# The wide weight sum s75 of block 1's first MLP matrix, made by a plain load and an accumulating DMA instead of VectorE

## The chip, the cores and the metric

The kernel runs on one core of a Trainium2 chip. The metric is the device time of one execution in microseconds (us). The kernel before took 1544.16 us, the median of three executions (1543.84 to 1545.23). Five engines work side by side, each in the order of its own queue: PE (matmul), DVE (VectorE), ACT (ScalarE), POOL (GpSimd) and SP, which here only issues transfers. They wait for each other by semaphores.

## The reference

Two blocks of a small transformer-like model run one after the other on 512 tokens of 1024 channels, each followed by a normalization. Block 1 is a mixer, an attention to a memory and an MLP; block 2 has a sliding-window attention, a convolution and a gated MLP. The part that the change touches is the MLP of block 1:

```
def squared_relu_mlp(h, w1, w2):
    return jnp.square(jax.nn.relu(h @ w1)) @ w2      # w1 1024 x 4096, w2 4096 x 1024
...
x = x + squared_relu_mlp(rmsnorm(x, norm_ffn[l]), ffn_w1[l], ffn_w2[l])
```

All of it is in float32.

## The kernel before, in words

Activations lie transposed, as eight tiles of 128 channels by 512 tokens. A float32 product is made of three products of a narrower format, fp32r: the operand is split into a high part (a cast on ACT) and a low part (the rest, a subtraction on DVE), and PE multiplies high by high, high by low and low by high (`mm3`, lines 459 to 463). The weights come in a fixed order as units of 512 KB, 128 partitions by 1024, eight tiles of 128 by 128. A unit is loaded by SP into a `raw` buffer (four of them; lines 242 and 269), cast by ACT into `whi` (258, 305) and subtracted by DVE into `wlo` (260, 262, 310); there are five buffers each of `whi` and `wlo`, and a cast waits until PE is done with the tile whose buffer it takes.

The first MLP matrix w1 has 16 column pairs. Two are multiplied plainly. The other fourteen, pairs 2 to 15, use Strassen's scheme in Winograd's form, with seven half-sized products in place of eight (`pairg`, `SEVEN`). One pair is two units, r0 and r1 (`wraw[u]` and `wraw[u+1]`). Some of the seven products need sums of blocks of the weights:

- s75 is r0 plus the second half of r1, added to both halves of r0: one DVE instruction on 128 by 1024 (`s75`, line 297), written to a buffer with the tag `sraw`, of which there are two (`NSR`);
- s64, on 128 by 512 twice, is made from s75 and r0 (`s6`, line 315), and from that and r1 (`s4`, line 318), into the other `sraw`.

Then r0 ("a"), s75, s64 and the first half of r1 ("b") are each split into high and low. `seven_steps` lists these operations as six steps. While PE works on an earlier unit, `sevens` hands them out, one step every two tiles of weights (`SPREAD`); what is late is put in by `pairg` at the pair's start. This is the order in which the program is written; where several engines are free to differ, a scheduler sets the order of each engine from it. SP's order is the order of the program.

At a pair's end one product bank is copied by ACT (`c0`, line 380), DVE makes four sums with the PSUM banks into `q` (386 to 389), ACT applies relu and the square (1355, 1356) and casts the result (1358), and DVE makes its low part (1363). The second matrix w2 is multiplied as soon as w1's columns are there. DVE scales its result out of PSUM (1391, `tmp`), and POOL adds it to the running sum (1393, `res+=tmp`).

The pairs are taken so: plain 0 and 1; 2, 3 and 4 together; four columns of w2; pair 5; four of w2; 6, 7 and 8; four of w2; 9; four of w2; 10, 11 and 12; four; 13; four; 14 and 15; eight. Pair 4, 8 and 12 are each the last of three pairs in a row. In the profiled execution this stage runs from 395 to 716 us.

Of the kernel before, what the change touches and what calls it, by code (L numbers as in the profile page):

```python
# [9 lines left out]
F32 = mybir.dt.float32  # L10
# [4 lines left out]
ALU = mybir.AluOpType  # L15
AX = mybir.AxisListType

P = 128
T = 512
D = 1024  # L20

NSLOT = 67
NRAW, NWS = 4, 5

NSR, NQ = 2, 2


SPREAD = [6, 2]
# [140 lines left out]
def _build(ctx, tc, nc, A, out, stage):  # L169
# [8 lines left out]
    def nm(s):  # L178
        cnt[0] += 1
        return f"{s}_{cnt[0]}"  # L180
# [48 lines left out]
    order, seven = weight_order()  # L229
# [44 lines left out]
    def sevens(u, later):  # L274


        if u not in sevp:
            load_raw(u, 1)
            sevp[u] = seven_steps(u)
        n = SPREAD[0] if later else len(sevp[u][1])  # L280
        todo = sevp[u][1]
        for j in range(min(n, len(todo))):
            if later:
                defer(SPREAD[1] * j, lambda todo=todo: todo and todo.pop(0)())
            else:
                todo.pop(0)()

    def seven_steps(u):
        r0, r1 = wraw[u], wraw[u + 1]
        wd = lambda dt, tag, b: wp.tile([P, 1024], dt, tag=tag, bufs=b, name=nm(tag))  # L290
        r3 = r0.rearrange("p (a b) -> p a b", a=2)
        op = {}
        t = {}

        def s75():
            t["s75"] = wd(F32, "sraw", NSR)
            V.tensor_tensor(t["s75"].rearrange("p (a b) -> p a b", a=2), r3,
                            r1[:, T:].unsqueeze(1).to_broadcast([P, 2, T]), op=ALU.add)

        def hi(n, src):  # L300
            def f():
                s = src()
                w = s.shape[-1]
                t[n] = (wd(F32R, "whi", NWS), wd(F32R, "wlo", NWS)) if w > T else (t2(F32R), t2(F32R))
                S.copy(t[n][0], s)  # L305
            return f

        def lo(n, src):
            def f():
                V.tensor_sub(t[n][1], src(), t[n][0].bitcast(F32))  # L310
            return f

        def s6():
            t["s64"] = wd(F32, "sraw", NSR)
            V.tensor_add(t["s64"][:, :T], t["s75"][:, T:], r0[:, :T])

        def s4():
            V.tensor_add(t["s64"][:, T:], t["s64"][:, :T], r1[:, :T])

        def both(*fs):  # L320
            def f():
                for g in fs:
                    g()
            return f

        def end():
            h = lambda n, j: tuple(a[:, j * T:(j + 1) * T] for a in t[n])
            op.update({1: h("a", 0), 4: h("a", 1), 7: h("s75s", 0), 5: h("s75s", 1),
                       6: h("s64s", 0), 3: h("s64s", 1), 2: t["b"]})

        a, b = (lambda: r0), (lambda: r1[:, :T])
        c, d = (lambda: t["s75"]), (lambda: t["s64"])
        return op, [
            both(s75, hi("a", a)),
            both(lo("a", a), hi("s75s", c)),
            both(s6, s4),
            both(lo("s75s", c), hi("s64s", d)),
            both(hi("b", b), lo("s64s", d)),
            both(lo("b", b), end),
        ]  # L340
# [5 lines left out]
    def pairg(name, n1, n2, ops, then, kind="mm"):  # L346
# [11 lines left out]
        wraw.pop(u)  # L358
        wraw.pop(u + 1)
        load_raw(u + 2, 3)  # L360
        if u + 2 in seven:
            sevens(u + 2, True)
        else:
            defer(7, lambda: prefetch(u + 2, 0, 0))
# [77 lines left out]
    def nxt(name, k, n, c=1):  # L442
# [4 lines left out]
        if i % 8 == 0:  # L447
            wraw.pop(u - 1, None)
            wsp.pop(u - 1, None)
            prefetch(u, *PF)  # L450
            if u + 2 in seven and u + 1 not in seven:
                sevens(u + 2, True)
        hi, lo = wsp[u]
# [1415 lines left out]
```

## Time and profile before

| | |
|---|---|
| median of three executions | 1544.16 us |
| the profiled execution | 1543.86 us, of which the span 1542.1 us |
| PE busy | 1514.8 us, 98% of the span |
| DVE busy | 999.0 us, 65% |
| ACT busy | 674.9 us, 44% |
| POOL busy | 143.5 us, 9% |
| loads of weights | 259 of 512 KB, 3.7 us from issue to landing (median) |

The profile is taken from one execution. Busy time is the sum of an engine's instructions, where matmuls that overlap count once; the time between the span and the execution's own time lies before the first and after the last instruction. The chain that ended last is followed back from the last instruction, at each step to what released it. Releasers are worked out from semaphore events: a wait stands under the one that came last.

### The profile page before, as it was taken

The numbers are of one execution on the slowest core, as the hardware profiler recorded it, in microseconds if no ns is written. First come the engines' busy times: TensorE is split into PE (matmuls) and PEld (weight loads), VectorE is DVE, ScalarE is ACT, GpSimd is POOL, SyncE is SP. The second block draws the span as 40 slices with busy tenths as digits, with TensorE's granted clock in tenths as the row PEclk, the third lists the DMA queues.
The fourth block names the chain that finished last, engine by engine and source line by source line (L and its number), as shares of the span: only waits on it lengthen the run. The fifth ranks groups of instructions, "written<-read, shape, count | busy, mean of one in ns | idle before, by whom it ended". The sixth has DMA issues, their size and how long they took to land.

```text
span 1542.1 us, 20324 instructions
## 1 busy us (share of the span) xinstructions
PE 1514.8 (98%) x7904; PEld 1274.9 (83%) x7904; DVE 999.0 (65%) x1623; ACT 674.9 (44%) x1117; POOL 143.5 (9%) x162
## 2 busy tenths in 40 slices
PE   8999999999999999999999999999999999999996
PEld 6888898888888888989888888888888888888886
DVE  6897675554786786767688767335546555555557
ACT  6666555443564353535444444333334331332233
POOL 0002120200201212011400000000020002001101
PEclk9999999999999999999999999999999999999998
DMA  6033335221223323324043222222232222232311
GB/s 254 20 111 100 112 130 197 96 68 55 82 72 106 96 95 109 104 83 137 14 150 131 83 82 83 81 92 92 92 96 96 96 96 96 96 96 92 100 41 56
DMA packets 51505, 149.89 MB, mean 97 GB/s; under 512 B 9552, under 2 KB 14032, under 8 KB 51408
## 3 DMA queue, kind: packets, MB, share of 16 engines
q1 hardware_dynamic: 51264, 148.32, 29.1%
q8 instruction: 62, 1.02, 0.3%
q14 instruction: 35, 0.29, 0.1%
q10 hardware_dynamic: 144, 0.26, 0.1%
HBM read 143.97 MB, written 3.28 MB: 95 GB/s over the span
## 4 chain that ended last, share of the span: by engine, by line
PE 95%; DVE 2%; ACT 2%; issue 1%; DMA 0%; POOL 0%; SPq 0%; DVEq 0%; ACTq 0%; POOLq 0%
PE mm L461 28%; PE mm L462 27%; PE mm L463 27%; PE sm L463 2%; PE sm L461 2%; PE sm L462 2%; ACT whi L258 0%; ACT t L1090 0%; DVE wlo L260 0%; DMA raw<-wts 0%; PE sm L581 0%; PE sm L1576 0%; PE sm L1575 0%; PE sm L1577 0%; PE sm L713 0%
## 5 line engine op out<-in xcount | busy, mean ns | idle before, releaser
L461 PE MATMUL mm<-t,whi 128*128 128x512 f32 (+1 forms) x1888 | 719.9, 381 | 9.1 <-ACT whi L254 7.3
L462 PE MATMUL mm<-t,whi 128*128 128x512 f32 (+1 forms) x1888 | 716.7, 380 | 0.2 <-DVE t L530 0.2
L463 PE MATMUL mm<-t,wlo 128*128 128x512 f32 (+1 forms) x1888 | 716.8, 380 | 0.0
L258 ACT CAST whi<-raw 128x1024 fp32r<-128x1024 f32 x226 | 236.5, 1051 | 432.7 <-PE mm L462 286.2
L461 PEld LDWEIGHTS mm<-t,whi 128*128 128x128 f32 x1888 | 355.3, 188 | 77.9 <-ACT whi L254 7.3
L463 PEld LDWEIGHTS mm<-t,wlo 128*128 128x128 f32 x1888 | 355.3, 188 | 72.1 <-DVE wlo L260 0.8
L462 PEld LDWEIGHTS mm<-t,whi 128*128 128x128 f32 x1888 | 355.2, 188 | 69.6 <-DVE t L530 0.4
L260 DVE TENSOR_TENSOR wlo<-raw,whi 128x1024 fp32r<-128x1024 f32 x219 | 287.4, 1312 | 81.8 <-ACT whi L258 78.8
L575 POOL TENSOR_TENSOR acc<-acc,tmp 128x512 f32<-128x512 f32 (+1 forms) x37 | 52.7, 1432 | 468.2 <-ACT tmp L571 467.9
L1436 DVE TENSOR_TENSOR tmp<-mm,acc 128x512 f32<-128x512 f32 x46 | 31.7, 689 | 48.8 <-PE mm L463 46.8
L1393 POOL TENSOR_TENSOR res<-res,tmp 128x512 f32<-128x512 f32 x24 | 39.0, 1638 | 247.9 <-DVE tmp L1391 217.3
L310 DVE TENSOR_TENSOR wlo<-sraw,whi 128x1024 fp32r<-128x1024 f32 x28 | 38.4, 1375 | 26.5 <-ACT whi L305 26.5
L461 PE MATMUL sm<-t,whi 128*128 128x256 f32 (+1 forms) x176 | 50.4, 286 | 1.8 <-ACT whi L305 1.8
L1676 DVE TENSOR_TENSOR zp<-mm,acc 128x512 f32<-128x512 f32 x22 | 15.2, 691 | 55.0 <-PE mm L463 54.9
L463 PE MATMUL sm<-t,wlo 128*128 128x256 f32 (+1 forms) x176 | 50.4, 286 | 0.0
L462 PE MATMUL sm<-t,whi 128*128 128x256 f32 (+1 forms) x176 | 50.2, 285 | 0.0
L305 ACT CAST whi<-sraw 128x1024 fp32r<-128x1024 f32 x28 | 29.3, 1047 | 45.8 <-PE mm L462 41.0
L1692 POOL TENSOR_TENSOR res<-res,tmp 128x512 f32<-128x512 f32 x16 | 20.7, 1294 | 260.2 <-DVE tmp L1691 260.2
L1679 DVE TENSOR_TENSOR tmp<-tmp,mm 128x512 f32<-128x512 f32 x22 | 15.1, 687 | 43.4 <-PE mm L463 42.6
L1391 DVE TENSOR_TENSOR tmp<-mm,acc 128x512 f32<-128x512 f32 x32 | 21.6, 686 | 26.5 <-PE mm L463 22.6
L1691 DVE TENSOR_TENSOR tmp<-mm,acc 128x512 f32<-128x512 f32 x16 | 11.1, 692 | 39.2 <-PE mm L463 39.2
L461 PEld LDWEIGHTS sm<-t,whi 128*128 128x128 f32 x176 | 33.1, 188 | 2.5 <-ACT whi L305 2.0
(379 smaller groups left out, 1840.2 us busy)
## 6 DMA issues: line engine op xcount, KB each, us to landing
raw<-wts SPq DMA_DIRECT2D x259, 512.0 KB, 3.7
res<-xT SPq DMA_DIRECT2D x16, 256.0 KB, 5.2
yT<-t SPq DMA_DIRECT2D x6, 256.0 KB, 2.3
tmp<-tmp SPq DMA_DIRECT2D x20, 64.0 KB, 2.0
gm<-gm SPq DMA_DIRECT2D x4, 256.0 KB, 5.2
dn<-ch SPq DMA_DIRECT2D x4, 256.0 KB, 2.3
tmp<-memT SPq DMA_DIRECT2D x4, 256.0 KB, 2.6
cst<-const SPq DMA_DIRECT2D x1, 576.0 KB, 6.7
```

Source lines behind the costliest of these rows:

```text
L258: S.copy(hi, r)
L260: defer(LO, lambda r=r, hi=hi, lo=lo: V.tensor_sub(lo, r, hi.bitcast(F32)))
L305: S.copy(t[n][0], s)
L310: V.tensor_sub(t[n][1], src(), t[n][0].bitcast(F32))
L461: PE.matmul(ps, lhsT=ahi, rhs=bhi, start=start, stop=False)
L462: PE.matmul(ps, lhsT=ahi, rhs=blo, start=False, stop=False)
L463: PE.matmul(ps, lhsT=alo, rhs=bhi, start=False, stop=stop)
L575: eng.tensor_add(acc[:, :w], acc[:, :w], dst[:, :w])
L1391: V.tensor_mul(t, ps, rb2)
L1393: G.tensor_add(x[n], x[n], t)
L1436: V.tensor_mul(t, ps, rb)
L1692: G.tensor_add(x[n], x[n], t)
```

## The change

The DVE instruction s75 is taken out. A new function `sums` makes s75 in a buffer of its own tag (two buffers, `NS75`): SP loads unit u a second time, now into s75, and POOL's queue issues a DMA that reads the second half of unit u+1 from memory twice (a broadcast of 512 columns to two halves) and adds it to what is there. `sums` is called where the pair's raw units are first loaded, and ahead of that for the pairs that come next: in `pairg`, after the raw loads, for the next two pairs, and in `nxt` two or three units ahead. `sraw` is left with one buffer, for s64. The pool of 512-column slots has 65 tiles instead of 67, and the scratch space of descriptors for DMAs is doubled.

```diff
--- before.py
+++ after.py
@@ -19,10 +19,10 @@
 T = 512
 D = 1024
 
-NSLOT = 67
+NSLOT = 65
 NRAW, NWS = 4, 5
 
-NSR, NQ = 2, 2
+NSR, NS75, NQ = 1, 2, 2
 
 
 SPREAD = [6, 2]
@@ -276,6 +276,7 @@
 
         if u not in sevp:
             load_raw(u, 1)
+            sums(u)
             sevp[u] = seven_steps(u)
         n = SPREAD[0] if later else len(sevp[u][1])
         todo = sevp[u][1]
@@ -285,17 +286,23 @@
             else:
                 todo.pop(0)()
 
+    sum75 = {}
+
+    def sums(u):
+
+        if u not in sum75:
+            s = wp.tile([P, 1024], F32, tag="s75", bufs=NS75, name=nm("s75"))
+            nc.sync.dma_start(out=s, in_=A["wts"][u])
+            nc.gpsimd.dma_start(out=s.rearrange("p (a b) -> p a b", a=2),
+                                in_=A["wts"][u + 1][:, T:].unsqueeze(1).to_broadcast([P, 2, T]),
+                                accum_op=ALU.add)
+            sum75[u] = s
+
     def seven_steps(u):
         r0, r1 = wraw[u], wraw[u + 1]
         wd = lambda dt, tag, b: wp.tile([P, 1024], dt, tag=tag, bufs=b, name=nm(tag))
-        r3 = r0.rearrange("p (a b) -> p a b", a=2)
         op = {}
-        t = {}
-
-        def s75():
-            t["s75"] = wd(F32, "sraw", NSR)
-            V.tensor_tensor(t["s75"].rearrange("p (a b) -> p a b", a=2), r3,
-                            r1[:, T:].unsqueeze(1).to_broadcast([P, 2, T]), op=ALU.add)
+        t = {"s75": sum75.pop(u)}
 
         def hi(n, src):
             def f():
@@ -331,7 +338,7 @@
         a, b = (lambda: r0), (lambda: r1[:, :T])
         c, d = (lambda: t["s75"]), (lambda: t["s64"])
         return op, [
-            both(s75, hi("a", a)),
+            hi("a", a),
             both(lo("a", a), hi("s75s", c)),
             both(s6, s4),
             both(lo("s75s", c), hi("s64s", d)),
@@ -358,6 +365,9 @@
         wraw.pop(u)
         wraw.pop(u + 1)
         load_raw(u + 2, 3)
+        for v in (u + 2, u + 4):
+            if v in seven:
+                sums(v)
         if u + 2 in seven:
             sevens(u + 2, True)
         else:
@@ -448,6 +458,9 @@
             wraw.pop(u - 1, None)
             wsp.pop(u - 1, None)
             prefetch(u, *PF)
+            for v in (u + 2, u + 3):
+                if v in seven:
+                    sums(v)
             if u + 2 in seven and u + 1 not in seven:
                 sevens(u + 2, True)
         hi, lo = wsp[u]
@@ -1857,7 +1870,7 @@
     from concourse.bass_utils import run_bass_kernel_spmd
 
     arrays = layout(inputs)
-    nc = bacc.Bacc("TRN2", target_bir_lowering=False, num_devices=1, dynamic_dma_scratch_size=1024)
+    nc = bacc.Bacc("TRN2", target_bir_lowering=False, num_devices=1, dynamic_dma_scratch_size=2048)
     A = {n: nc.dram_tensor(n, a.shape, mybir.dt.from_np(a.dtype), kind="ExternalInput").ap()
          for n, a in arrays.items()}
     out = nc.dram_tensor("yT", (8, P, T), F32, kind="ExternalOutput").ap()
```

Lines after the edit are numbered otherwise: 297 is gone, 305 is 312, 310 is 317, 315 is 322, 318 is 325, 386 to 389 are 396 to 399, 1393 is 1406. The new load is line 295, the accumulating DMA line 296. The numbers in names count the tiles of the program, and the same tile can have a number one or two higher.

POOL's queue around pairs 10, 11 and 12 (s75_1152, s75_1170, s75_1175), after the change; `res` lines are the adds of w2's columns.

```order
L1406 TENSOR_TENSOR res_591_2840<-res_591_2840,tmp_1147_5799 128x512
L1406 TENSOR_TENSOR res_592_2842<-res_592_2842,tmp_1153_5836 128x512
L1406 TENSOR_TENSOR res_593_2844<-res_593_2844,tmp_1165_5884 128x512
L1406 TENSOR_TENSOR res_594_2846<-res_594_2846,tmp_1171_5922 128x512
L296 DMA s75_1175_5931<-wts 128x2x512
L296 DMA s75_1238_6340<-wts 128x2x512
L1406 TENSOR_TENSOR res_587_2832<-res_587_2832,tmp_1233_6331 128x512
L1406 TENSOR_TENSOR res_588_2834<-res_588_2834,tmp_1239_6368 128x512
L1406 TENSOR_TENSOR res_589_2836<-res_589_2836,tmp_1251_6416 128x512
```

Before, only the adds stood there. The accumulating DMA of pair 12 stands behind four adds, and that of pair 13 right behind it.

SP's queue at the same place after the change: raw_1172, raw_1173 and raw_1174 are loads of whole units, s75_1170 and s75_1175 the new plain loads of pairs 11 and 12.

```order
L295 DMA s75_1170_5894<-wts 128x1024
L269 DMA raw_1172_5925<-wts 128x1024
L269 DMA raw_1173_5927<-wts 128x1024
L269 DMA raw_1174_5929<-wts 128x1024
L295 DMA s75_1175_5931<-wts 128x1024
L269 DMA raw_1195_6052<-wts 128x1024
L269 DMA raw_1196_6054<-wts 128x1024
L269 DMA raw_1216_6181<-wts 128x1024
```

Before, the raw loads followed one another without the two between them.

DVE before, at pair 12: sraw_1197 is its s75, sraw_1203 its s64; sraw_1175 and sraw_1181 are those of pair 11, and q_1189 is pair 11's result.

```order
L310 TENSOR_TENSOR wlo_1180_5940<-sraw_1175_5920,whi_1179_5939 128x1024
L297 TENSOR_TENSOR sraw_1197_6044<-raw_1172_5915,raw_1173_5917 128x1024
L310 TENSOR_TENSOR t2_1187_5983<-raw_1171_5913,t2_1186_5982 128x512
L310 TENSOR_TENSOR wlo_1185_5971<-sraw_1181_5951,whi_1184_5970 128x1024
L315 TENSOR_TENSOR sraw_1203_6082<-sraw_1197_6044,raw_1172_5915 128x512
L318 TENSOR_TENSOR sraw_1203_6082<-sraw_1203_6082,raw_1173_5917 128x512
L386 TENSOR_TENSOR q_1189_6030<-mm_1183_5959,t2_1182_5957 128x2x256
L310 TENSOR_TENSOR wlo_1199_6047<-raw_1172_5915,whi_1198_6046 128x1024
L387 TENSOR_TENSOR q_1189_6030<-mm_1178_5937,q_1189_6030 128x512
L310 TENSOR_TENSOR wlo_1202_6069<-sraw_1197_6044,whi_1201_6068 128x1024
L388 TENSOR_TENSOR q_1189_6030<-mm_1178_5937,q_1189_6030 128x256
L389 TENSOR_TENSOR q_1189_6030<-mm_1188_5992,q_1189_6030 128x512
```

DVE after, at the same place: s75_1175 is pair 12's s75, sraw_1203 its s64, s75_1170 and sraw_1182 those of pair 11, and q_1190 pair 11's result.

```order
L317 TENSOR_TENSOR wlo_1181_5953<-s75_1170_5894,whi_1180_5952 128x1024
L317 TENSOR_TENSOR t2_1188_5996<-raw_1172_5925,t2_1187_5995 128x512
L317 TENSOR_TENSOR wlo_1186_5984<-sraw_1182_5964,whi_1185_5983 128x1024
L322 TENSOR_TENSOR sraw_1203_6093<-s75_1175_5931,raw_1173_5927 128x512
L325 TENSOR_TENSOR sraw_1203_6093<-sraw_1203_6093,raw_1174_5929 128x512
L396 TENSOR_TENSOR q_1190_6043<-mm_1184_5972,t2_1183_5970 128x2x256
L317 TENSOR_TENSOR wlo_1199_6058<-raw_1173_5927,whi_1198_6057 128x1024
L397 TENSOR_TENSOR q_1190_6043<-mm_1179_5950,q_1190_6043 128x512
L317 TENSOR_TENSOR wlo_1202_6080<-s75_1175_5931,whi_1201_6079 128x1024
L398 TENSOR_TENSOR q_1190_6043<-mm_1179_5950,q_1190_6043 128x256
L399 TENSOR_TENSOR q_1190_6043<-mm_1189_6005,q_1190_6043 128x512
L317 TENSOR_TENSOR wlo_1207_6113<-sraw_1203_6093,whi_1206_6112 128x1024
```

The line of 297 is gone. What follows stands in the same order: s6 (now line 322) behind the low part of pair 11's s64, and ahead of the four sums of pair 11's q.

ACT before, in the first triple: whi_923 is the high part of pair 3's s64, t2_903 the high part of pair 2's b.

```order
L1358 CAST t2_885_4195<-q_844_4054 128x512
L1358 CAST t2_887_4197<-q_844_4054 128x512
L305 CAST whi_923_4352<-sraw_920_4333 128x1024
L305 CAST t2_903_4254<-raw_891_4201 128x512
L1358 CAST t2_906_4286<-q_889_4199 128x512
L1358 CAST t2_908_4288<-q_889_4199 128x512
L380 COPY t2_921_4339<-mm_913_4296 128x256
```

ACT after, at the same place (whi_924 and t2_903).

```order
L1371 CAST t2_886_4198<-q_844_4054 128x512
L1371 CAST t2_888_4200<-q_844_4054 128x512
L312 CAST t2_903_4255<-raw_892_4204 128x512
L312 CAST whi_924_4357<-sraw_921_4338 128x1024
L1371 CAST t2_907_4290<-q_890_4202 128x512
L1371 CAST t2_909_4292<-q_890_4202 128x512
L390 COPY t2_922_4344<-mm_915_4303 128x256
```

The two casts have changed places: b's high part now comes ahead of that of s64.

## Rows read from the trace of the kernel before

**Rows 1.** The head of the page: the span; its part 1, busy time, share of the span and instructions of each engine; of part 2 the row of the granted clock, in tenths of full speed in 40 slices; of part 4 the shares of the engines in the chain that ended last.

```profile
span 1542.1 us, 20324 instructions
...
PE 1514.8 (98%) x7904; PEld 1274.9 (83%) x7904; DVE 999.0 (65%) x1623; ACT 674.9 (44%) x1117; POOL 143.5 (9%) x162
...
PEclk9999999999999999999999999999999999999998
...
PE 95%; DVE 2%; ACT 2%; issue 1%; DMA 0%; POOL 0%; SPq 0%; DVEq 0%; ACTq 0%; POOLq 0%
```

**Rows 2.** The table of stretches: from:to in us, length, then the busy time of PE, of its weight loads (PEld), of DVE, ACT and POOL with their instructions, the granted clock, the mean busy share of the DMA engines, GB/s. Four of eleven stretches of block 1's MLP in which PE is busy for less than the length, one between them, the sum of all eleven, and a stretch of block 2.

```profile
434.00:443.00 9.00, 7.28 (x55) 6.71 (x54) 8.65 (x14) 8.18 (x14) 0.00 (x0) 1.00 0.16 57
443.00:460.00 17.00, 17.00 (x144) 16.92 (x143) 15.14 (x19) 9.35 (x13) 0.00 (x0) 1.00 0.31 99
460.00:471.00 11.00, 9.15 (x70) 8.57 (x69) 9.35 (x13) 6.40 (x10) 0.00 (x0) 1.00 0.54 184
...
545.00:556.00 11.00, 10.36 (x82) 9.94 (x81) 8.77 (x12) 6.67 (x10) 0.00 (x0) 1.00 0.61 213
...
629.00:640.00 11.00, 10.32 (x87) 10.12 (x86) 8.77 (x12) 7.19 (x11) 0.00 (x0) 1.00 0.53 180
...
sum 321.00, PE 316.11 PEld 281.65 DVE 240.53 ACT 153.15 POOL 44.83; mean PE 28.74 PEld 25.61 DVE 21.87 ACT 13.92 POOL 4.08
...
760.00:900.00 140.00, 139.82 (x690) 116.33 (x690) 109.12 (x205) 61.22 (x112) 2.50 (x11) 1.00 0.33 105
```

**Rows 3.** The waits of PE between 380 and 720 us, by what ended them: total us, times, longest.

```profile
PE sm L461 <- ACT whi L305: 1.8, 1, 1.8
PE mm L461 <- ACT t L305: 1.5, 1, 1.5
PE mm L461 <- ACT t L380: 1.3, 2, 0.7
PE mm L462 <- DVE t L530: 0.2, 1, 0.2
```

**Rows 4.** The sum s75 of line 297: its group on DVE in the MLP (busy us, mean ns of one, idle time ahead of it and what ended that), and the durations of the fourteen in ns (least/median/most), with the first and last start.

```profile
L297 DVE TENSOR_TENSOR sraw<-raw,raw 128x1024 f32<-128x1024 f32 x14 | 18.1, 1291 | 17.2 <-DMA raw<-wts 17.2
...
L297 DVE TENSOR_TENSOR sraw<-raw,raw x14: 1216/1223/2199, 401.9 to 683.0; 128x1024 f32<-128x1024 f32 x14
```

**Rows 5.** Timelines (start in us, duration, engine, line, operation, out<-in, and in brackets the idle time ahead with what ended it): ACT, DVE and PE at the first three pairs, 403 to 444 us, and PE and ACT at 468 to 470.

```profile
438.26 1.14 ACT L1358 CAST t<-q 128x512 fp32r<-128x512 f32 x2
439.50 1.04 ACT L305 CAST whi<-sraw 128x1024 fp32r<-128x1024 f32 x1
440.45 0.61 ACT L305 CAST t<-raw 128x512 fp32r<-128x512 f32 x1
...
403.60 1.22 DVE L260 TENSOR_TENSOR wlo<-raw,whi 128x1024 fp32r<-128x1024 f32 x1
...
437.51 1.22 DVE L297 TENSOR_TENSOR sraw<-raw,raw 128x1024 f32<-128x1024 f32 x1
...
441.72 0.68 DVE L310 TENSOR_TENSOR t<-raw,t 128x512 fp32r<-128x512 f32 x1
...
442.92 1.29 DVE L1363 TENSOR_TENSOR t<-q,t 128x512 fp32r<-128x512 f32 x2
...
407.30 0.40 PE L463 MATMUL mm<-t,wlo 128*128 128x512 f32 x1
...
441.12 0.39 PE L461 MATMUL mm<-t,t 128*128 128x256 f32 x1 [1.54 <-ACT t L305]
...
469.58 0.39 PE L461 MATMUL sm<-t,whi 128*128 128x256 f32 x1 [1.83 <-ACT whi L305]
...
468.49 1.04 ACT L305 CAST whi<-raw 128x1024 fp32r<-128x1024 f32 x1
```

**Rows 6.** Transfers: part 6 of the page (KB of one, median us from issue to landing) and the row of queue q1 in part 3 (packets, MB, time as a share of 16 engines' span); the landings of the loads by line 269 in the MLP; and the issues of single loads on SP's queue (start, duration).

```profile
raw<-wts SPq DMA_DIRECT2D x259, 512.0 KB, 3.7
...
q1 hardware_dynamic: 51264, 148.32, 29.1%
...
DMA to landing us min/median/max: 3.5/3.8/4.8
...
393.16 0.33 SPq L242 DMA_DIRECT2D raw<-wts  x1
...
432.98 0.33 SPq L269 DMA_DIRECT2D raw<-wts  x1
...
521.41 0.33 SPq L269 DMA_DIRECT2D raw<-wts  x1
...
523.11 0.33 SPq L269 DMA_DIRECT2D raw<-wts  x1
...
608.24 0.33 SPq L269 DMA_DIRECT2D raw<-wts  x1
```

**Rows 7.** Two of POOL's 24 adds `res+=tmp`, from its timeline.

```profile
525.02 1.30 POOL L1393 TENSOR_TENSOR res<-res,tmp 128x512 f32<-128x512 f32 x1 [2.49 <-ACT whi L305]
...
611.18 2.14 POOL L1393 TENSOR_TENSOR res<-res,tmp 128x512 f32<-128x512 f32 x1 [1.82 <-DVE tmp L1391]
```

**Rows 8.** Timelines of DVE and ACT at the third pair of the second and of the third triple (pairs 8 and 12).

```profile
532.16 0.69 DVE L315 TENSOR_TENSOR sraw<-sraw,raw 128x512 f32<-128x512 f32 x1
...
616.07 1.23 DVE L310 TENSOR_TENSOR wlo<-sraw,whi 128x1024 fp32r<-128x1024 f32 x1 [1.06 <-ACT whi L305]
...
622.58 0.69 DVE L389 TENSOR_TENSOR q<-mm,q 128x512 f32<-128x512 f32 x1
...
623.31 1.15 ACT L1355 ACTIVATE q<-q 128x512 f32<-128x512 f32 x2 [3.08 <-DVE q L389]
...
634.24 1.15 ACT L1355 ACTIVATE q<-q 128x512 f32<-128x512 f32 x2 [3.78 <-DVE q L389]
...
639.32 0.36 ACT L380 COPY t<-mm 128x256 f32<-128x256 f32 x1
```

## The prediction, on record before the result

> **What bounds the kernel now.** I read the page's head first [rows 1]: the matrix engine PE is busy for 1514.8 of 1542.1 us, the clock was granted in full in nearly every slice, and PE carries 95% of the chain that ended last. So a change that takes work off VectorE (DVE) wins only where PE stands idle because of DVE. The second view is the table of stretches of block 1's MLP, 395 to 716 us, where all fourteen sums stand [rows 2]: PE is busy for 316.11 of 321.00 us. The missing 4.89 us lie in four stretches: 9.00 − 7.28 = 1.72, 11.00 − 9.15 = 1.85, 11.00 − 10.36 = 0.64 and 11.00 − 10.32 = 0.68. More than 4.9 us can't be won here. Third, the waits of PE [rows 3]: all but 0.2 us of them end with a ScalarE (ACT) instruction, a hi cast or the copy of c0, none with a sum. Fourth, the sums themselves [rows 4]: 14 of 1.29 us, 18.1 us of DVE in all, and ahead of them DVE waited 17.2 us for the second raw unit to land, without one PE wait naming it. So most of what is removed was hidden. The fifth view, the timelines of DVE and ACT, shows where it isn't hidden, and where a late sum would be felt.
>
> **What goes.** The only place where a sum stands in front of PE's wait is the first triple, 437 to 441 us [rows 5]. PE waits 1.54 us for the hi part of pair 2's b, an ACT cast that ran at 440.45 because the 1.04 us cast at 439.50 stood ahead of it. In the new order of ACT the two change places. b's cast then runs near 439.4, after the two casts that begin at 438.26 and take 1.14. Its lo part on DVE, at 441.72 before, moves with it, since the 1.22 us sum of 437.51 is gone from DVE. That saves about 1.0 us; the bounds are 0 and the whole 1.7 of the two waits in this stretch [rows 3]. The wait at 469.58 (1.83) ends with the hi cast of a raw unit at 468.49, which no sum feeds [rows 5], and the two of 1.3 us together, near 555 and 640, end a chain that I follow below; none of these goes because a sum goes. The 17.2 us of DVE waits go too, and what is late next is s6 of the same pair.
>
> **What is added.** Fourteen plain 512 KB loads on SP's queue (0.33 us of SP each) and fourteen accumulating DMAs on POOL's. q1 moved 148.32 MB in 29.1% of the span [rows 6], so 512 KB keep the 16 engines busy for about 0.291 × 1542.1 × 0.524 / 148.32 = 1.6 us. The traffic by itself is 14 × 2 × 1.6 = 45 us of DMA time in 321 us whose busiest stretch so far is at 0.61 [rows 2]; I cost it at nothing. If the raw units came late by it, each late unit would be a PE stall of the same length. SP's queue hands the plain load out among the raw loads, so a raw unit behind it moves back by one issue step, 523.11 − 521.41 = 1.7 us [rows 6]. DVE's waits for a raw unit, 17.2 us in all, did not reach PE [rows 3, 4], so I cost this at nothing too.
>
> What is not hidden is when s75 is ready. Before, it took DVE 1.22 us once both raw units lay there. Now it takes the plain load's issue (1.7 after the raw load ahead of it), its landing, and then L, the time from POOL's issue to the accumulating DMA's landing. For the plain landing I take 4.5 us, between the median 3.8 and the longest 4.8 of the loads by line 269 [rows 6], since it is always the second or third of a burst.
>
> No row shows L. From below it is a plain load of the same bytes, 3.7 us. From above: two more passes of 1.6 us for reading the destination and writing it back, and POOL held by DVE for twice the 2.14 us that its add took beside DVE work [rows 7], so 3.7 + 3.2 + 4.3 = 11.2. I take 6.3: one pass more for reading the destination, and 1.0 for an issue that costs POOL what its shortest add costs (1.30, against SP's 0.33). That is nearer to the plain load, the only DMA row of this size.
>
> The Trainium skill, "DMA: Bandwidth & Descriptors", section on the anatomy of one DMA on the GpSimd path, puts such a DMA at 2.0 us plus bytes over 436 GB/s, 3.2 us here; it speaks of plain ones, and the plain loads of this trace take 3.7 on the other path. With 3.2 for L the sum below would be −1.0 + 0.3, no change. No row here shows that path.
>
> **Where a late s75 is paid.** DVE keeps its order, so it stands still at s6, the first reader, and everything behind waits, q adds and lo parts alike. s6 is paid at four pairs, those whose loads go out late because they close or open a triple.
> - Pair 12. The raw load ahead went out at 608.24 [rows 6]; plain load 609.9, landed 614.4, ready 614.4 + L. s6 stands right behind the lo part that ends at 617.30 [rows 8]. The stall is L − 2.9, 3.4 us at 6.3. Behind it stand the q adds of pair 11 up to 622.58; ACT had waited 3.08 us for the last of them and then worked without a gap worth naming, through DVE's second set of q adds (ACT waits 3.78) to c0 at 639.32, for which PE waited 0.68 [rows 3, 8]. So the stall is paid one for one. POOL is free by then (611.18 + 2.14 = 613.3 [rows 7]).
> - Pair 8, the same chain one triple earlier: raw 521.41, plain 523.1, landed 527.6, ready 527.6 + L; s6's place 532.1, where it ran [rows 6, 8]; POOL is free from 526.3 [rows 7]. Stall L − 4.5, 1.8 us, on the chain that ends in the 0.64 wait.
> - Pair 4: raw 432.98, plain 434.7, landed 439.2; s6 now stands behind the two t's that ended at 442.92 + 1.29 = 444.2 [rows 5]; with the sum gone from ahead of them I put its place at 443.7. Stall L − 4.5, 1.8 us. Behind it are a lo part and q adds that PE wants some us later; no wait of PE stood between 443 and 460 [rows 2]. Ends 0 and 1.8; I take a third, 0.6.
> - Pair 2: raw 393.16, plain 394.9, landed 399.4. s6 now stands ahead of the lo part of a plain unit that ran at 403.60. That lo part ends at 399.4 + L + 0.68 + 1.22, and PE reads it near 407.30 [rows 5]: price L − 6.0, 0.3 us.
> The other ten either have their loads out several us earlier or wait under a PE that isn't due: 0.
>
> Sum: −1.0 + 3.4 + 1.8 + 0.6 + 0.3 = +5.1 us. The profiled execution took 1543.86 us, span 1542.1 and 1.8 around it, 0.3 below the median of 1544.16. So 1549.0 beside that execution, 1549.3 beside the median. With the low end of L the four are 0.8, 0, 0 and 0, and the sum is −0.2; with the high end 8.3, 6.7, 2.2 and 5.2, +21.4; the sum crosses zero near L = 4.
>
> **The other edits.** Two tile slots fewer change the order of ACT and DVE in block 2's attention, where PE was idle for 0.18 of 140 us [rows 2]; I take 0, with a gain of 0.2 at most and, if a slot is late, a price of some us. One sraw buffer instead of two holds only s64 now, whose last reader stands ahead of the next s6 on DVE: 0. POOL's adds now stand behind accumulating DMAs that wait for a plain landing; POOL is busy for 9% of the span [rows 1], and its sums are read by its own later adds and after the MLP: 0.
>
> **Rivals.** (1) *A fast accumulate*: L of 3.7 to 5.5 us. s75 comes in the shadow of work, pair 12 alone pays 0.8 to 2.6, and the sum is −0.2 to +2.9: 1544 to 1547. For it speaks that the DMA queues were idle 70% of the time; against it that the destination must be read as well.
> (2) *A slow one*: L of 8.7, two passes more and POOL's issue held once beside DVE (3.7 + 3.2 + 1.8). The four pay 5.8, 4.2, 1.4 and 2.7, the sum is +13.1: 1557. For it speaks that DVE and POOL hold each other up in this trace: the same POOL add took 1.30 us and 2.14, the same DVE sum 1.22 and 2.20 [rows 4, 7]. The Trainium skill, "SBUF — State Buffer", section on the doors and who blocks whom, says the same of a DMA issued from GpSimd: its descriptors can't be written while DVE holds the pair of ports they share, and the DMA starts late. By that rule this rival, not mine, is the likely one; the trace agrees on the adds and shows no such DMA.
> (3) *Faster*: DVE, lighter by 18.1 us, reaches the q adds earlier, ACT's chains start earlier, and beside the 1.0 the 1.8 at 469.6 and the two of 0.65 shrink too. All of it gone is −4.9, 1539.0; half is −2.45, 1541.4. For it: the waits are real. Against it: in those chains DVE waited for ACT and PE, not for a sum [rows 8]. It needs L below 4 at pair 12.
> (4) *The change costs elsewhere*: the smaller pool stalls block 2 by 4 us with L harmless: 1548.
>
> **How the numbers follow.** Mine, L between 5.5 and 8: 0.38, +2.9 to +10.8, 1547 to 1555. The fast accumulate 0.33; slow 0.13; faster 0.11; the pool 0.05. What a measurement of this kernel can tell from no change is 0.2%, 3.1 us. L is above 5.5 in nearly all of the first and all of the slow case, so slower is 0.38 × 0.95 + 0.13 + 0.04 = 0.53; faster by over 3.1 us needs two thirds of all idle time, 0.09; the rest is no change, 0.38. The range, 1542 to 1557.5, holds my case, the fast one and half of the slow one and of the faster one.
>
> **What would show it.** In the changed kernel: the time from the accumulating DMA's issue to its landing (6.3, within 3.7 to 11.2); DVE idle ahead of line 322, ended by a DMA into s75, about 3.4 us near 617, 1.8 near 532 and 445; PE's wait for c0's copy grown from 0.68 to about 4 near 640 and from 0.64 to 2.4 near 555; the wait at 441 shrunk to about 0.5; that at 469.6 unchanged. I am wrong in mechanism if these DVE waits are there and PE's are not, or if PE loses time outside 395 to 716; wrong in size if L lies elsewhere.

## The result and the profile after

The changed kernel took 1561.17 us (median of four executions, 1560.17 to 1563.34), the kernel before 1544.0 beside it: 1.0111 times as long, with a 95% interval of 1.0095 to 1.0127. So it is slower, as forecast, but by 17.2 us where the prediction had 5.1, and outside its range, which ended at 1557.5. The profiled execution took 1560.17 us with a span of 1558.4, 16.3 more than before.

First the page of the changed kernel: the span, part 1, the chain, and the two rows of part 6 on the new transfers. They answer to [rows 1] and [rows 6].

```profile
span 1558.4 us, 20399 instructions
...
PE 1522.2 (98%) x7904; PEld 1279.8 (82%) x7904; DVE 980.0 (63%) x1609; ACT 674.0 (43%) x1117; POOL 161.6 (10%) x176
...
PE 85%; DVE 5%; DMA 3%; ACT 3%; issue 2%; POOL 1%; SPq 0%; DVEq 0%; ACTq 0%; POOLq 0%
...
s<-wts SPq DMA_DIRECT2D x14, 512.0 KB, 5.2
s<-wts POOLq DMA_DIRECT2D x14, 512.0 KB, 7.3
```

DVE is 19 us lighter, as planned, and it brought nothing: PE's share of the chain fell from 95% to 85%, and transfers into `s` (s75) have 3% of it, where DMA had none. An accumulating DMA takes 7.3 us to land. PE's own busy time grew by 7.4 us for the same 7904 products. That is a second loss beside the waits, and the forecast had no term for it.

Of the table of stretches, columns as in [rows 2], two rows and the sum. The times are those of the changed kernel, which runs 4 us late against the one before at 545 and 15 at the end of the MLP; 640 to 735 holds the end of the triple of pair 12.

```profile
556.00:608.00 52.00, 47.05 (x238) 39.93 (x238) 30.94 (x42) 18.39 (x25) 8.78 (x7) 0.97 0.52 140
...
640.00:735.00 95.00, 91.63 (x541) 81.48 (x540) 60.68 (x71) 43.63 (x58) 17.24 (x11) 0.96 0.48 144
sum 340.00, PE 325.69 PEld 289.06 DVE 224.09 ACT 154.42 POOL 62.35; mean PE 29.61 PEld 26.28 DVE 20.37 ACT 14.04 POOL 5.67
```

PE idles for 340.00 − 325.69 = 14.31 us in the MLP, 9.4 more than before. In the two stretches shown the granted clock is below 1.00, which it was in no stretch of the MLP before. The rest of the 16.3 us, 16.3 − 9.4 = 6.9, is not idle time: PE takes longer for the same products.

PE's waits in the MLP of the changed kernel (380 to 740 us), to be held against [rows 3]:

```profile
PE mm L474 <- ACT t L312: 4.6, 3, 2.7
PE sm L476 <- DVE t L317: 2.0, 1, 2.0
PE mm L474 <- ACT t L390: 1.8, 1, 1.8
PE sm L474 <- ACT whi L312: 1.8, 1, 1.8
PE mm L476 <- DVE t L317: 1.6, 2, 0.9
PE sm L630 <- DVE t L543: 1.4, 1, 1.4
PE sm L474 <- ACT t L312: 1.1, 1, 1.1
```

No wait names a transfer. Read alone, this view says that ACT and DVE are too slow. One step further back stands what makes them late, in the waits ahead of s6 (line 322 now) and of the accumulating DMA:

```profile
  DMA s<-wts: 43.4, 10
...
  DMA s<-wts: 93.2, 10
...
L296 POOL DMA_DIRECT2D s<-wts x14: 1194/1204/1332, 398.3 to 696.5; - x14
...
DMA to landing us min/median/max: 5.7/7.3/9.2
```

The first line is s6's: DVE stood still 43.4 us for s75, at ten of fourteen pairs. At an eleventh, pair 4, the view puts 1.8 us under "issue", but s75 landed there just before s6 began (445.13 and 445.21). The other lines are those of the accumulating DMA: POOL waited for the plain load to land, issued the DMA in 1.2 us (ns, least/median/most), and it landed 5.7 to 9.2 us after the issue began. Not every standstill reaches PE: the two longest, 7.0 us at pair 10 and 6.5 at pair 14, have no PE wait behind them.

### The profile page after: what moved, and what is told of

It reads as the page before. It is cut to its first block, busy times and chain, and to the rows that moved or that the text cites. A ratio compares the mean times of both kernels' runs of the same rounds, so it can differ in the third digit from the quotient of the medians.

```text
span 1558.4 us, 20399 instructions
## 1 busy us (share of the span) xinstructions
PE 1522.2 (98%) x7904; PEld 1279.8 (82%) x7904; DVE 980.0 (63%) x1609; ACT 674.0 (43%) x1117; POOL 161.6 (10%) x176
## 4 chain that ended last, share of the span: by engine, by line
PE 85%; DVE 5%; DMA 3%; ACT 3%; issue 2%; POOL 1%; SPq 0%; DVEq 0%; ACTq 0%; POOLq 0%
PE mm L474 25%; PE mm L476 25%; PE mm L475 25%; DMA s<-wts 3%; PE sm L474 2%; PE sm L476 2%; PE sm L475 2%; DVE wlo L317 1%; POOL res L1406 0%; ACT whi L312 0%; ACT t L1103 0%; ACT q L1368 0%; DVE wlo L260 0%; DVE t L1376 0%; DVE t L317 0%
## 5 line engine op out<-in xcount | busy, mean ns | idle before, releaser
L1449 DVE TENSOR_TENSOR tmp<-mm,acc 128x512 f32<-128x512 f32 x46 | 31.7, 689 | 48.3 <-PE mm L476 46.3
L1368 ACT ACTIVATE q<-q 128x512 f32<-128x512 f32 x28 | 16.1, 623 | 64.7 <-DVE q L399 64.7
L322 DVE TENSOR_TENSOR sraw<-s,raw 128x512 f32<-128x512 f32 x14 | 9.7, 692 | 45.2 <-DMA s<-wts 43.4
L1704 DVE TENSOR_TENSOR tmp<-mm,acc 128x512 f32<-128x512 f32 x16 | 11.1, 691 | 39.2 <-PE mm L476 39.2
L474 PE MATMUL mm<-t,t 128*128 128x256 f32 x108 | 31.2, 290 | 4.6 <-ACT t L312 4.6
```

The lines of the kernel that those rows point to most:

```text
L474: PE.matmul(ps, lhsT=ahi, rhs=bhi, start=start, stop=False)
L1368: S.activation(q[:, j * T:(j + 1) * T], q[:, j * T:(j + 1) * T], AF.Relu, scale=1.0 - 2 * j)
L1449: V.tensor_mul(t, ps, rb)
```

## The experiments

Three theories. A: s75 is late, DVE and ACT stand still for it in their order, PE runs dry. B: the second load and the accumulating DMA cost by their traffic. C: the smaller pool of slots or the single buffers stall something. The first four kernels tell them apart.

**e1: the same memory, sums on DVE.** s75 is allocated under the changed kernel's tag (one buffer), the rest of its memory stays, `sums` issues nothing.

```diff
...
-        t = {"s75": sum75.pop(u)}
...
+        def s75():
+            t["s75"] = wd(F32, "s75", 1)
+            V.tensor_tensor(t["s75"]..., r3, r1[:, T:]..., op=ALU.add)
```

> The changed kernel's memory (65 slots, one buffer for s64, one for s75, the larger descriptor scratch), but all fourteen sums made by VectorE again and no extra DMA. Theory A (s75 comes late, and DVE and ACT stand still for it): nothing is late here, so 1543 to 1545.5 us, no difference from before, and PE idle in block 1's MLP of about 4.9 us as before. Theory B (the second load and the accumulating DMA get in the way of other work by their traffic): the same, 1543 to 1545.5. Theory C (the smaller pool or the single buffer stalls): most of the 17 us stay, 1555 or more.

1545.68 us (11 runs), 1.0012 times the kernel before, interval 1.0003 to 1.0021. PE's waits in the MLP are those of [rows 3] within 0.2 us. C has at most 1.7 of the 17 us, and no wait of PE in the MLP, as long as nothing else is late there.

**e2: e1 and the transfers, for nobody.** `sums` fills a buffer `dummy` that no instruction reads.

```diff
-            s = wp.tile([P, 1024], F32, tag="s75", bufs=NS75, ...)
+            s = wp.tile([P, 1024], F32, tag="dummy", bufs=1, ...)
...
```

> e1, and beside it the fourteen plain loads and fourteen accumulating DMAs of the change, in the same places of SP's and POOL's queues, into a buffer that nobody reads. What is left of the loss is the price of the transfers alone. Theory A: nobody waits for them, so at most 2 us over e1, 1543 to 1547; the accumulating DMA still takes about 7 us to land. Theory B: the loss comes back without a reader, 1552 to 1561.

1546.30 us, 1.0016 (1.0008 to 1.0025), 0.6 over e1. The transfers landed as in the changed kernel (4.8 and 6.8 us, medians), so they were really there. B falls: a second load of 7.3 MB, fourteen DMAs on POOL and their 7.3 MB cost nothing that can be told from e1 where nobody waits for them.

**e3: the plain load alone.** The accumulating DMA is taken out, so the sum lacks the second half of r1.

```diff
-            nc.gpsimd.dma_start(out=s..., in_=A["wts"][u + 1]..., accum_op=ALU.add)
```

> The changed kernel without the accumulating DMAs: s75 is the plain load alone, so the second half of r1 is left out of the sum. Readers wait for the plain load only, some 7 to 9 us earlier. Theory A: s75 is ready before s6's place at pairs 4 and 8, some us late at none but perhaps pair 9 or 12 (plain load of pair 12 landed 2.8 us ahead of s6's place, of pair 9 with nothing to spare); DVE's waits ahead of line 322 fall from 43 us to under 8, 1542.5 to 1546, no clock below 1.00 in the MLP. Theory B, by its half (the plain loads stay): 1548 to 1555.

1544.80 us, 1.0007 (0.9998 to 1.0016). What DVE waited for ahead of s6, which is line 319 of this kernel:

```profile
  DMA s<-wts: 9.7, 4
```

So s6 still stands still, 9.7 us in place of 43.4 (under 8 was expected), at pairs 5, 6, 10 and 14 for the plain load alone. None of it reaches PE. PE's wait near 440, 1.54 in [rows 3], is 0.30, and no other is longer than before. So this is what s75 in time brings: 1.2 us at that place, not more than the smaller pool costs. One expectation was missed: the clock fell below 1.00 once in the profiled execution, between 460 and 480 us (last section).

**e4: the same transfers, earlier.** `pairg` asks for the s75 of the next two pairs, before the raw loads, as soon as its own buffer is free.

```diff
+        for v in sorted(seven, key=int):
+            if u < v and len([w for w in seven if u < w <= v]) <= 2:
+                sums(v)
         load_raw(u + 2, 3)
-        for v in (u + 2, u + 4):
-            if v in seven:
-                sums(v)
```

> The changed kernel with s75 of each pair asked for two pairs ahead (as soon as its buffer is free), ahead of the raw loads in SP's queue: the same transfers, only earlier. Theory A: the waits ahead of line 322 go but for pair 2, which is loaded where it was; PE idle falls from 14.3 us to 3 to 5 and the clock holds, 1541.5 to 1546. Theory B: the same traffic costs the same, 1555 to 1562. A raw load that is held behind a plain load waiting for its buffer would show as PE waits on line 258's or 312's casts with a DMA behind them.

1546.16 us, 1.0010 (1.0001 to 1.0019): 15 of the 17.2 us are gone with every byte still moved. PE's waits in e4, and what DVE waited for ahead of s6:

```profile
PE sm L474 <- ACT whi L312: 1.9, 1, 1.9
PE mm L474 <- ACT t L312: 1.1, 1, 1.1
PE mm L474 <- ACT t L390: 1.1, 2, 0.6
...
  DMA raw<-wts: 12.9, 6
  DMA s<-wts: 3.3, 1
```

The accumulating DMAs take 5.8 to 10.2 us as before, but only one is waited for (pair 2's, whose place didn't move). PE idles for 4.2 us in the MLP, as expected; the clock did not hold, though, but fell once at 470 us (last section). Theory A stands: not the price of the sum in a DMA is the loss, but the moment at which it is asked for.

The next kernels ask how the loss is shared out.

**e5, e6: one pair alone.** `sums` issues its transfers for pair 9 (e5) or pair 12 (e6) only; DVE makes the other thirteen, in the same buffers.

```diff
+        if sorted(seven).index(u) + 2 not in (9,):
+            sum75[u] = None
         if u not in sum75:
...
```

> Only pair 9's sum is made by the load and the accumulating DMA, at the change's place; VectorE makes the other thirteen in the same buffers. Beside e1 (1545.7): if the loss is a sum over pairs, pair 9 alone brings its 3.1 us of PE idle (the two waits at 585 and 587 us of the changed kernel) and about 2 us of slower clock behind them, 1549.5 to 1552.5. If pair 9's waits need the delay that pairs 4 and 8 had brought before it, PE idles little here, 1545 to 1548.

> Only pair 12's sum by the load and the accumulating DMA. By the sum over pairs: VectorE stands still for 4 to 6 us at s6, PE idles 2.5 to 3.5 us in all where it idled 0.6, and the clock falls behind it for 2 to 2.5 us more, 1549.5 to 1552. If VectorE's stall were paid one for one, as I had forecast, 5 us of idle alone. If the clock falls only after several waits in a row, 1547.5 to 1549.

e5 1552.01 us (1.0050, 1.0038 to 1.0062), e6 1551.81 (1.0046, 1.0034 to 1.0058): 6.3 and 6.1 us over e1 from one pair each, by the medians. Not all of that need be the pair's: in both profiles the clock also falls at 470 us, long before either pair, for a loss of 1.7 us that e1's profile doesn't have (last section). e5's runs lie widely, 1549.0 to 1555.3; its profile is of one at the low end (1549.64 us), with 2.3 us of idle at pair 9, where 3.1 was expected, and no fall of the clock behind it. The four runs above 1551 have a lower mean clock (0.994 or 0.995, against 0.996 and 0.997 in the other two), so it fell more often there; where, no profile shows. In e6's profile the waits and the clock are these (PE's waits between 620 and 650 us, then stretches with the granted clock third from the end):

```profile
PE mm L483 <- ACT t L321: 2.5, 1, 2.5
PE mm L485 <- DVE t L326: 0.9, 1, 0.9
...
630.00:640.00 10.00, 6.53 (x44) 6.12 (x43) 7.19 (x10) 6.40 (x10) 0.00 (x0) 0.87 0.26 90
640.00:650.00 10.00, 9.65 (x62) 8.70 (x62) 7.84 (x11) 6.35 (x9) 0.00 (x0) 0.96 0.43 151
```

3.5 us of idle in the first of these stretches, and behind it between 6.53 × 0.13 + 9.65 × 0.04 = 1.2 us and 10 × 0.13 + 10 × 0.04 = 1.7 us of PE work lost to the clock. DVE's standstill of 4.6 us at s6 became 3.5 us of idle, so it is not paid one for one.

**e7: all but pair 9.**

```diff
+        if sorted(seven).index(u) + 2 not in (2, 3, 4, 5, 6, 7, 8, 10, 11, 12, 13, 14, 15):
+            sum75[u] = None
         if u not in sum75:
```

> The changed kernel with pair 9's sum alone back on VectorE. If the loss is a sum over pairs, its 5 us go: 1555 to 1557.5 against 1561.2, the waits at 585 and 587 and the slower clock behind them are gone, those at pairs 8 and 12 stay. If pair 9's place is taken by another wait in the same stretch, 1558 or more.

1558.08 us (four runs, 1.0087, 1.0073 to 1.0102): 3.1 us less than the changed kernel, where pair 9 alone had cost 6.3. The idle time of pair 9 is gone: PE's waits in the MLP come to 11.4 us in e7's profile, 2.9 less than in the changed kernel's. But in this profile, of the longest of its runs (1561.26), the clock is at 0.83 in three stretches where the changed kernel's held at 1.00 (450 to 460, 470 to 480, 560 to 570 us). So far as these profiles show, the idle time adds up over the pairs and the clock's loss does not.

**e8: what the landing time is made of.** Pairs of extra transfers, nearly all in block 2, read by nobody, in several forms; four of them:

```diff
+            nc.gpsimd.dma_start(out=s, in_=A["wts"][u])
+            nc.gpsimd.dma_start(out=s, in_=A["wts"][u + 1], accum_op=ALU.add)
...
+            nc.gpsimd.dma_start(out=s3, in_=wide)
+            nc.gpsimd.dma_start(out=s3, in_=wide, accum_op=ALU.add)
```

> e1 with extra transfers in block 2 that nobody reads, in pairs of six forms, to take the landing time apart: on POOL's queue a plain 512 KB load, the same with the broadcast, accumulating without and with the broadcast, accumulating 256 KB; on SP's the plain load with and without the broadcast. If reading the destination costs a second pass, accumulating takes about 1.6 us or more over plain on the same queue, and 256 KB clearly less than 512. If the path through POOL is what costs, plain on POOL takes as long as accumulating, 6 us or more. If the broadcast's shorter pieces cost, both broadcast forms are longer than those without. Time 1545 to 1549.

The landings of e8, one form after the other: on POOL's queue plain; accumulating; plain with the broadcast; accumulating with the broadcast, the change's form; on SP's queue plain; and on POOL's accumulating 256 KB without the broadcast.

```profile
DMA to landing us min/median/max: 4.4/5.0/6.1
...
DMA to landing us min/median/max: 6.6/7.6/8.5
...
DMA to landing us min/median/max: 3.8/4.2/7.3
...
DMA to landing us min/median/max: 5.4/5.8/8.2
...
DMA to landing us min/median/max: 4.5/4.6/5.2
...
DMA to landing us min/median/max: 4.9/5.5/5.7
```

Accumulating adds 1.6 us with the broadcast (4.2 to 5.8) and 2.6 without (5.0 to 7.6); I had put 1.6, one more pass, from q1's row. Half the bytes, without the broadcast, land 2.1 us sooner (7.6 to 5.5). Both fit a second pass over the destination and don't prove it. The queue through POOL adds 0.4 us to SP's 4.6 and not 1.0; the plain load on it takes 5.0 us, not the 3.2 that the prediction quotes. The broadcast makes a transfer on POOL's queue shorter, by medians of six whose ranges overlap; on SP's it does not (4.8, against 4.6). So the change's form takes 5.8 us here and 7.3 in the MLP. What the other 1.5 are was not tried. In the traces the landing is longest where most other transfers are under way: 9.2 us at pair 9, beside three loads of weights and one from ACT's queue (9.5 at the same place in e2), and 6.0 at pair 14, beside one load. The time, expected at 1545 to 1549, was 1566.17 us (two runs). POOL stood still for hundreds of us behind the extra transfers; what that holds up in block 2 was not followed.

**e9, e10: the smaller pool.** The kernel before with NSLOT = 65 (e9), and with the descriptor scratch of 2048 besides (e10).

```diff
-NSLOT = 67
+NSLOT = 65
```

> The kernel before with 65 slots in place of 67 and nothing else, to see where e1's 1.7 us over before come from. If the smaller pool costs them: 1545 to 1546.5. If they come from the separate buffers of s75 and s64 or from the descriptor scratch: 1543.5 to 1544.5.

> e9 with the descriptor scratch of the change as well. No theory has it cost time: the same as e9 within 0.8 us. If it does, e1's 1.7 us appear here and not in e9.

1547.28 us (1.0014, 1.0005 to 1.0023) and 1545.43 us (1.0008, 0.9999 to 1.0017). The two differ by 1.9 us, more than expected, though their runs cover the same stretch (1545.3 to 1547.9 and 1544.8 to 1547.9). Times of one kernel lie in two groups (last section): eight of e9's eleven runs lie in the upper one, three of e10's. Group beside group, both are 0.9 to 1.4 us over the kernel before, so this is what the pool costs, and the scratch costs nothing that can be told. No PE wait in their traces is longer for it. In e10 the delay comes up evenly between 1170 and 1460 us, where PE is busy throughout (the load that SP issues at 1167.5 us before goes out at 1167.6, the one of 1456.4 at 1457.8); by what, stays open.

One wait of DVE in the MLP is longer with 65 slots. DVE's waits for POOL, in the kernel before and in e9:

```profile
DVE t L310 <- POOL res L1393: 0.6, 2, 0.3
...
DVE t L310 <- POOL res L1393: 1.7, 2, 1.4
```

The 1.4 us stand ahead of the low part of pair 9's b (577.74 in e10, 579.97 in e9). It takes one of the 512-column slots, and so does `tmp`, which POOL's add must have read first. PE doesn't wait for this low part in e9, e10 or e1. In the changed kernel it does.

No version here beats the kernel before.

## Why the prediction was wrong, point by point

**What holds.** PE sets the time and is only late where DVE and ACT are late; the sums were hidden; the traffic costs nothing by itself (e2); DVE stands still at s6, and the price is on the chain from there to PE. The triples' last pairs pay, as named. The gain near 440 is there, but smaller: b's cast ran at 439.44, as forecast, yet PE waited 1.24 us in place of 1.54, not 0.5. Here the late s75 of pair 2 shows, behind which all of DVE and ACT came later: the wait is 1.14 in e4, where only pair 2's s75 is still waited for, and 0.30 in e3, where it is not.

**The balance, term by term.** The forecast had −1.0 for the gain, 3.4 for pair 12, 1.8 for pair 8, 0.6 for pair 4, 0.3 for pair 2, nothing for the others and nothing for the clock. PE's idle time changed by −0.3 near 440, by 2.74 + 0.63 − 0.68 = 2.7 at pair 12, by 0.58 + 0.92 + 1.84 − 0.64 = 2.7 at pair 8, by 1.4 at pair 4 (near 448) and by 1.12 + 1.99 = 3.1 at pair 9; a wait of 0.2 near 438 is gone. That is the 9.4 us. The places that were named come to 6.5, near the forecast of 5.1. What had been put at nothing, pair 9 and the clock, took it out of the range.

**The failing step: "The other ten either have their loads out several us earlier or wait under a PE that isn't due: 0."** PE idles 3.1 us at pair 9, more than at pair 12, and alone it makes the kernel about as slow as pair 12 alone (e5, e6). Its chain in the changed kernel: POOL's issue, s6 on DVE, the end of the piece of ACT work ahead of b's cast, that cast, b's low part on DVE, and PE's two waits.

```profile
556.46 1.21 POOL L296 DMA_DIRECT2D s<-wts  x1 [25.67 <-DVE wlo L260]
...
565.73 0.69 DVE L322 TENSOR_TENSOR sraw<-s,raw 128x512 f32<-128x512 f32 x1 [5.68 <-DMA s<-wts]
...
583.65 0.63 ACT L1353 ACTIVATE acc<-tmp 128x512 f32<-128x512 f32 x1 [1.69 <-DVE tmp L1351]
584.32 0.62 ACT L312 CAST t<-raw 128x512 fp32r<-128x512 f32 x1
...
586.73 0.69 DVE L317 TENSOR_TENSOR t<-raw,t 128x512 fp32r<-128x512 f32 x1 [1.38 <-POOL res L1406]
...
584.99 0.39 PE L474 MATMUL sm<-t,t 128*128 128x256 f32 x1 [1.12 <-ACT t L312]
587.48 0.39 PE L476 MATMUL sm<-t,t 128*128 128x256 f32 x1 [1.99 <-DVE t L317]
```

What POOL waited for was the plain load, not the DVE line that the bracket names: it went out at 549.88 and landed at 555.78, 5.9 us later, and POOL began 0.7 us behind the landing. The accumulating DMA took 565.73 − 556.46 = 9.3 us, the longest of all. The first half of the forecast's sentence was wrong for pair 9, too. In the kernel before, the load ahead of its place and its s6 stand here:

```profile
545.55 0.33 SPq L242 DMA_DIRECT2D raw<-wts  x1
...
558.48 0.68 DVE L315 TENSOR_TENSOR sraw<-sraw,raw 128x512 f32<-128x512 f32 x1
```

By the forecast's own terms s75 would be ready at 545.55 + 1.7 + 4.5 + 6.3 = 558.05. That is 0.4 us to spare and not several.

I had asked when PE wants s75 and s64 of this pair, and it is indeed late in wanting them. But DVE and ACT keep their order, and between s6 and b's cast there stand the relu of pair 8 and the preparation of block 2's rotary tables (lines 1331 to 1354), a chain that goes to and fro between DVE and ACT with 5.0 and 1.7 us of ACT waits. Most of the 5.7 us stall went through all of it to b's cast. In the kernel before, b's cast ran at 575.61:

```profile
575.61 0.61 ACT L305 CAST t<-raw 128x512 fp32r<-128x512 f32 x1
```

It moved by 8.7 us. The work itself was some 4.7 us late by then (the first q add of pair 8 began at 554.7 before and at 559.4 now), so 4 us were left, more than the slack. At the end of the chain the smaller pool adds its part. b's cast ended at 584.94, but its low part waited until 586.73 for POOL's add, 1.38 us, as it does with 65 slots in e9 too. So by this chain 1.4 of the 3.1 us come from the two slots fewer, which the forecast had put at 0; the change with 67 slots was not run.

**Two sizes that were wrong and cancelled: pairs 8 and 12.** The forecast had L = 6.3, stalls of 1.8 and 3.4 us, and PE paying them in full. s6 of pair 8 and of pair 12 in the changed kernel, with POOL's issues ahead of them, and PE's waits that follow at pair 12:

```profile
529.59 1.20 POOL L296 DMA_DIRECT2D s<-wts  x1 [0.89 <-DMA s<-wts]
...
536.13 0.69 DVE L322 TENSOR_TENSOR sraw<-s,raw 128x512 f32<-128x512 f32 x1 [3.40 <-DMA s<-wts]
...
624.18 1.20 POOL L296 DMA_DIRECT2D s<-wts  x1
...
631.89 0.69 DVE L322 TENSOR_TENSOR sraw<-s,raw 128x512 f32<-128x512 f32 x1 [5.55 <-DMA s<-wts]
...
643.87 0.58 PE L474 MATMUL mm<-t,t 128*128 128x256 f32 x1 [2.74 <-ACT t L312]
...
645.30 0.58 PE L476 MATMUL mm<-t,t 128*128 128x256 f32 x1 [0.63 <-DVE t L317]
```

L was 6.5 at pair 8 and 7.7 at pair 12. For pair 12 the formula L − 2.9 gives 4.8, and 5.55 was measured. The way from the raw load's issue, at 618.62, to POOL's was not longer than assumed (5.6 us, against 1.7 + 4.5). But the raw load itself went out 7.7 us ahead of s6's place (631.89 − 5.55 = 626.34), and before it was 617.30 − 608.24 = 9.1; why it was later I did not follow. I took the stall to be paid at c0, at the end of the chain. PE felt it sooner, at b's cast, which had some slack: a stall of 5.55 became 2.74 + 0.63 us of idle, and the wait for c0 (0.68 before) went. At pair 8 the stall of 3.40 became waits of 0.58 and 0.92 for b and 1.84 for c0, where 0.64 had been. So longer stalls were paid in smaller part, and that the two pairs together come to 5.4 us, against a forecast of 5.2, is luck.

**What had no term: the clock.** Behind pair 9's and pair 12's waits PE itself was slower. Four stretches of 4 us of the changed kernel (the granted clock is third from the end; 1.00 is 2.4 GHz, 0.50 is 1.2):

```profile
584.00:588.00 4.00, 1.03 (x6) 0.82 (x7) 2.62 (x4) 1.85 (x3) 1.26 (x1) 1.00 0.41 133
588.00:592.00 4.00, 4.00 (x24) 4.00 (x24) 1.25 (x2) 1.13 (x2) 1.28 (x1) 0.61 0.83 275
...
644.00:648.00 4.00, 3.37 (x14) 3.07 (x15) 3.96 (x6) 0.77 (x1) 0.00 (x0) 0.50 0.55 177
648.00:652.00 4.00, 4.00 (x27) 4.00 (x26) 1.46 (x3) 2.97 (x4) 0.00 (x0) 0.71 0.90 325
```

In 584 to 588 PE was busy for 1.03 us, then the clock fell to its lower level for most of the next 4 us; the same behind 643. The loss in these three slow rows is 4 × 0.39 + 3.37 × 0.50 + 4 × 0.29 = 4.4 us. With 9.4 of idle that is 13.8. Of the remaining 2.5 of the 16.3 us, some 1.3 may be what the smaller pool costs in e1, e9 and e10 outside the MLP; the rest stays open.

**The rivals.** The slow accumulate (1557) was nearest in time, but not by its cause: POOL's issue took 1194 to 1332 ns in all fourteen cases, so no row shows DVE holding it up. The Trainium skill, "SBUF — State Buffer", sections "SBUF: two separate sides" and "Who interferes with whom", has such an issue starved while DVE runs an instruction in a two-port mode, and says that tensor_tensor has no such mode. Beside the fourteen issues of this trace DVE ran tensor_tensor (eight) or nothing (six), so the prediction was mistaken to call this rival the likely one by that rule. The fast accumulate and the gain by a lighter DVE are refuted by the 7.3 us and by e3. (The sum given for the fast one, up to +2.9, holds 1.3 us of pairs 8 and 4 at its upper end, though its sentence says that pair 12 alone pays.) The smaller pool is real but small alone, and dearer where s75 is late (pair 9).

## What to carry to other kernels

An engine's instruction that is replaced by a DMA turns a duration into a latency: the two landings here, one behind the other, took some 12 us (5.2 + 7.3) in place of 1.2, so ask for it as many us earlier, or leave it where it is (e4 against the change: 15 us apart with the same transfers). When a value comes late, follow the whole queue behind its first reader, on each engine, until PE; that the value itself is wanted late says nothing of what stands behind it. Of eleven standstills here five came through to PE (pairs 2, 4, 8, 9 and 12), and not the longest ones. And where PE waits, price the clock behind the wait as well.

## What the runs showed of the hardware that was not expected

The clock fell also behind a wait that all these kernels share, the 1.8 us near 469 us, in some executions and not in others. The profiles of e2, e3, e4, e5, e6, e7 and e9 show it; those of the kernel before, the changed kernel, e1 and e10 don't. The stretch of 470 to 480 us in e9, and then in e10:

```profile
470.00:480.00 10.00, 10.00 (x38) 8.12 (x38) 6.79 (x10) 3.89 (x7) 0.00 (x0) 0.83 0.32 107
...
470.00:480.00 10.00, 10.00 (x45) 8.10 (x44) 7.42 (x11) 4.20 (x6) 0.00 (x0) 1.00 0.33 107
```

PE got through 38 products there in place of 45, and 10 × 0.17 = 1.7 us were lost. The times of most of these kernels lie in two groups about 2 us apart (the kernel before beside e9: 1543.4 to 1544.8 in 16 of 21 runs, 1545.9 to 1546.7 in five), which fits: the mean granted clock of a whole execution is 0.996 in these five and 0.997 or 0.998 in the sixteen. Where in them it fell only a profile shows. A difference under 2 us between such kernels is partly a matter of how many runs fell on each side: e4's four runs of the lower group, 1543.7 to 1544.8, are level with the kernel before, and its median of 1546.16 lies in the upper one.
